# A hybrid encoder trunk on one core: weight-sum transfers issued behind bias rows, one convolution tile's taps behind the key selection, and the last scaling reordered

## The chip, the cores and the metric

The kernel runs on one core of a Trainium2 chip. The metric is the device time of one execution in microseconds, the median of several runs. The core has five engines that work side by side, each through its own queue in order: PE (TensorE, matrix products), DVE (VectorE, elementwise work), ACT (ScalarE, functions such as tanh and exp), POOL (GpSimd, here mostly the issuer of transfers) and SP (SyncE, also an issuer of transfers). SBUF is the on-chip memory, PSUM holds the results of matrix products, DRAM is the memory off the core. 16 DMA engines carry all transfers.

## The reference

The input is 512 positions of width 2048, with 16 meta tokens in front, so 528 columns. Two residual layers follow, each behind an RMS norm, and a final RMS norm whose gain is one number per channel.

```python
# even layer: one projection, two groups of heads
u = glu_v * sigmoid(glu_g)                       # 1024 channels
u = causal_depthwise_conv(u, width 31) + conv_b  # 31 taps per channel
a_out = silu(layer_norm(u)) * silu(gate_a)
score = sum_h wi * relu(qi_h . ki)               # 16 indexer heads
keys  = top 128 admissible keys per query        # chunk-causal
p     = softmax(q_lat . c + relative bias, over the selected keys)   # 8 heads
b_out = (p c w_uv) * silu(gate_b)
h = h + concat(a_out, b_out) @ w_out
# odd layer: gated linear recurrence, 16 heads, then h = h + (...) @ w_out
out = rms_norm(h, final_norm_gain)[16:]
```

## The kernel before

Activations lie in SBUF with channels on the 128 partitions and positions along the free dimension, so a width of 2048 is 16 tiles. A product is done three times to keep precision (high part with high part, high with low, low with high: L177, L178, L179). Weights come as blocks of 512 KB, loaded by SP (L144), and are split into a high part on ACT (L148) and a low part on DVE (L149). A projection of 128 output channels is a "stripe"; its result stands in PSUM (three buffers named mps) and is moved out by DVE with the norm's factor (`evac`, L185).

The order of each engine's queue is fixed when the program is built. A planner simulates the program and issues what is ready by priority bands: weight preparation, then evictions, then side work (scores, selection, attention), then the convolution, then all else in the order of the text. `issue_after(x)` adds a tie: what the block issues on x's own engine is queued behind x.

**Even layer.** The list `EVEN` (L46) gives the order of the text. `g` is a convolution tile: two stripes, the gated input u (L550, two buffers), then 31 taps on DVE (L554 and 30 times L556), each over 528 columns. `s` is one tile of two indexer heads: a stripe, two transfers of query halves by POOL (L506), small products, and DVE adds the weighted scores to four masks (L520). `k` is the selection for one block of 128 queries, on DVE: 16 times a maximum of eight and a replacement (L528, L529), then the mask is written (L530, L531). `h` is one attention head: two stripes, then `attend`. `n` is the layer norm over the eight convolution tiles.

**Attention.** For each of four query blocks `softmax` takes a tile L (three buffers). POOL loads the bias rows into it (L578), and adds the mask by an accumulating transfer (L580), which waits until the rows have landed and the mask is there. PE makes the logits (L587), DVE adds L and finds the extreme (L589), ACT takes the exponential and the scaling (L593, L596), PE transposes (L605, L609), ACT copies (L606, L610), and PE multiplies by the values (L612). A fifth, small block of 16 meta positions has bias rows of 1 KB and no mask.

**Weight sums.** The output projections use a seven-product form that needs sums of weight blocks. These are made by transfers in DRAM: `copy` steps and accumulating `add` steps of 512 KB each. For the even layer 16 copies (`plain_steps`) go out on SP during `g` and `s`; 48 further steps (`steps`: 16 first adds, then copies and adds, L247 and L249) go out on POOL during the heads.

**End.** The odd layer's output projection runs in 56 turns of 24 products. `add` puts results onto the residual h2; `finish` squares a finished half tile on ACT (L1114) and adds the square into a running sum (L1117). When all 16 tiles of the first half of the positions are complete, `final(0)` makes the norm's factor rsp in PSUM and scales tile by tile on DVE (L1151: h2 times the channel's gain times rsp), in four groups of four tiles. The groups stand between later turns by an order written out by hand (`tail`): two groups at once, one after the third last turn, one after the second last. `final(1)` follows after the last turn with all 16 tiles of the second half, through products, logarithm and exponential (L1131, L1132, L1134, L1136), and SP stores the output (L1153).

Of the kernel before, what the change touches and what calls it, by code (L numbers as in the profile page):

```python
# [14 lines left out]
AF = mybir.ActivationFunctionType  # L15
# [27 lines left out]
         "wiT": "ei", "ki": "ei", "rt": "ei", "m8": "ei",  # L43
         "mask0": "ei", "mask1": "ei", "mask2": "ei", "mask3": "ei"}

EVEN = "g0 s0 g1 s1 g2 s2 g3 s3 s4 s5 s6 s7 k0 k1 k2 k3 h0 h1 h2 g4 g5 h3 g6 h4 h5 g7 n0 h6 h7".split()  # L46

STAGE = [("gt", 3)] * 3 + [("gb", 2)] * 2 + [("qh", 2), ("mb", 2), ("mb", 2)]

# [23 lines left out]
def trunk_kernel(ctx: ExitStack, tc: tile.TileContext, x: bass.AP, w: bass.AP, wukv: bass.AP,  # L73
# [192 lines left out]
    def some_steps(todo, n, behind):  # L266
        with tc.issue_after(behind.ins):
            for _ in range(min(n, len(todo))):
                sum_step(*todo.pop(0))
# [224 lines left out]
    def scores(j):  # L494
        ps = stripe(S_QI + j, X0, wide=False)
        some_steps(plain_steps, 1, loaded[0])

        qab = E.tile([128, 2 * SEQ], F32R, name=("uh", "ul")[j % 2], bufs=1)
        qa, qb = qab[:, :SEQ], qab[:, SEQ:]
        ql = epools["ei"].tile([128, SEQ], F32R, name="ql", bufs=1)  # L500
        lo, up = slice(0, 64), slice(64, 128)
        with band(EVAC):
            for q, hi, lw, hf, other in ((qa, qa, ql, lo, up), (qb, ql, qb, up, lo)):
                S.activation(hi[hf], ps[0][0][hf], AF.Copy)
                V.tensor_tensor(lw[hf], ps[0][0][hf], hi[hf].bitcast(F32), op=OP.subtract)
                G.dma_start(q[other], ql[hf])  # L506
        with band(SIDE):
            for t in range(NB):
                for hh in range(2):
                    h, W = 2 * j + hh, wk(t)  # L510
                    q = (qa, qb)[hh]
                    qs = slice(128 * t, 128 * (t + 1))
                    for s0, s1 in (((0, W),) if W <= 512 else ((0, HT), (HT, W))):
                        p = ps1()
                        se = max(s1, s0 + 256)
                        P.matmul(p[:, :se - s0], q[:, qs], kih[:, s0:se], start=True, stop=False)  # L516
                        P.matmul(p[:, :se - s0], q[:, qs], kil[:, s0:se], start=False, stop=True)
                        r = et([128, T], F32, "sq", 3)
                        S.activation(r[:, :s1 - s0], p[:, :s1 - s0], AF.Relu)
                        V.scalar_tensor_tensor(M[t][:, s0:s1], r[:, :s1 - s0], wiT[:, t, h:h + 1],  # L520
                                               M[t][:, s0:s1], op0=OP.mult, op1=OP.add)

    def select(t):

        with band(SIDE):
            for _ in range(TOPK // 8):
                m8 = et([128, 8], F32, "m8", 2)
                V.max(m8, M[t])  # L528
                V.match_replace(M[t], m8, M[t], TAKEN)  # L529
            V.tensor_scalar(M[t], M[t], -2e38, NEG, op0=OP.is_gt, op1=OP.mult)  # L530
            V.memset(M[t][:64, wk(t) - 64:], NEG)  # L531


    Z = []
# [1 line left out]
    def glu(i):  # L536
        ps = stripe(S_GLU + 2 * i, X0)
        some_steps(plain_steps, 1, loaded[0])
        g = et([128, T], F32, "gt", 3)
        with band(EVAC):  # L540
            evac(g, ps, rstd0)
            S.activation(g, g, AF.Tanh, scale=0.5)
        ps = stripe(S_GLU + 2 * i + 1, X0)
        some_steps(plain_steps, 1, loaded[0])
        v = et([128, T], F32, "gt", 3)
        u = et([128, CW - 1 + T], F32, "u", 2)
        with band(EVAC):
            evac(v, ps, rstd0)
            V.memset(u[:, :CW - 1], 0.0)
            V.scalar_tensor_tensor(u[:, CW - 1:], g, 1.0, v, op0=OP.add, op1=OP.mult)  # L550
        z = et([128, T], F32, "z", 8)
        eng = V
        with band(CONV):
            eng.tensor_scalar(z, u[:, :T], col(V_CW + i * CW), col(V_CB + i), op0=OP.mult, op1=OP.add)  # L554
            for j in range(1, CW):
                eng.scalar_tensor_tensor(z, u[:, j:j + T], col(V_CW + i * CW + j), z,  # L556
                                         op0=OP.mult, op1=OP.add)
        Z.append(z)

    def gate(s, dst, X, rstd, wide=True):  # L560
# [12 lines left out]
    def attend(h, qh, gb, Kh, Vt):  # L573
        o = pso()

        def softmax(t, nq, q0, W):
            e = et([128, T], F32, "L", 3)
            G.dma_start(e[:nq, :W], bias_rows(h, q0, nq, 0, W))  # L578
            if t is not None:
                masked = G.dma_start(e[:, :W], M[t], accum_op=OP.add)  # L580
                some_steps(steps, 1 + t % 2, masked)
            L = e
            st = et([128, 4], F32, "st", 3)
            parts = ((0, W),) if W <= 512 else ((0, HT), (HT, W))
            for i, (s0, s1) in enumerate(parts):
                p = ps1()
                P.matmul(p[:nq, :s1 - s0], qh[:, q0:q0 + nq], Kh[:, s0:s1], start=True, stop=True)  # L587

                V.tensor_tensor_reduce(L[:nq, s0:s1], p[:nq, :s1 - s0], e[:nq, s0:s1], -1.0,  # L589
                                       st[:nq, i - 1:i] if i else BIG, OP.add, OP.min,  # L590
                                       st[:nq, i:i + 1])
            i = len(parts) - 1
            S.activation(L[:nq, :W], L[:nq, :W], AF.Exp, bias=st[:nq, i:i + 1], scale=-1.0,  # L593
                         accum_out=st[:nq, 2:3])
            V.reciprocal(st[:nq, 3:4], st[:nq, 2:3])
            S.activation(L[:nq, :W], L[:nq, :W], AF.Identity, scale=st[:nq, 3:4])  # L596
            return L

        for t in range(NB):
            q0, W = NM + 128 * t, wk(t)  # L600
            L = softmax(t, 128, q0, W)
            pt = et([128, 5, 128], F32, "pt", 2)
            p = ps1()
            for j in range(t + 1):
                P.transpose(p[:, j * 128:(j + 1) * 128], L[:, NM + 128 * j:NM + 128 * (j + 1)], ident)  # L605
            S.activation(pt[:, 1:t + 2, :], p[:, :128 * (t + 1)], AF.Copy)  # L606

            p = ps1()
            P.transpose(p[:, :128], L[:, :128], ident)  # L609
            S.activation(pt[:, 0, :], p[:, :128], AF.Copy)  # L610
            for j in range(t + 2):
                P.matmul(o[:, 128 * t:128 * (t + 1)], Vt[:, j, :], pt[:, j, :],  # L612
                         start=j == 0, stop=j == t + 1)
        mb = et([128, T], F32, "mb", 2)
        V.tensor_tensor(mb[:, NM:], o, gb[:, NM:], op=OP.mult)
        L = softmax(None, NM, 0, NM)
        p = ps1()
        P.transpose(p[:NM, :NM], L[:NM, :NM], ident[:NM, :NM])
        pt = et([128, 5, 128], F32, "pt", 2)
        V.tensor_copy(pt[:NM, 0, :NM], p[:NM, :NM])  # L620
        p = ps1()
        P.matmul(p[:, :NM], Vt[:NM, 0, :], pt[:NM, 0, :NM], start=True, stop=True)
        V.tensor_tensor(mb[:, :NM], p[:, :NM], gb[:, :NM], op=OP.mult)
        Q.dma_start(mbd[h], mb)
# [37 lines left out]

    for step in EVEN:
        what, i = step[0], int(step[1:])
        if what == "n":
            rz = layer_norm()
        else:
            {"g": glu, "s": scores, "k": select, "h": head}[what](i)


    MA = []
# [419 lines left out]
    acc2 = keep.tile([128, T], F32, name="rstd1", bufs=1)[:, :SEQ]  # L1091
    done = [0, 0]


    tail = []

# [7 lines left out]
    def finish(n, c):  # L1104

        cs = slice(c * HS, (c + 1) * HS)
        h2, a2 = H2[n][:, cs], acc2[:, cs]
        done[c] += 1
        sq = last = None
        if done[c] == 1:  # L1110
            S.activation(a2, h2, AF.Square)
        else:
            sq = tmp()
            last = S.activation(sq, h2, AF.Square)  # L1114
            if done[c] < KT:
                with tc.issue_after(tail[-1].ins) if tail else ExitStack():
                    ins = V.tensor_tensor(a2, a2, sq, op=OP.add)  # L1117
                if tail:
                    tail.append(ins)
        if done[c] == KT:  # L1120
            pending.append((sq, last))

    def final(c, behind=None):
# [14 lines left out]
        for g, size in enumerate((1, 1, 2, 2, 2, 2, 2, 2, 2) if c else (2,) * 8):  # L1138
# [9 lines left out]
            o = o[:, :size * HS].rearrange("p (n t) -> p n t", n=size)  # L1148
            with tc.issue_after(tail[-1].ins) if c == 0 and g else ExitStack():
                for i in range(size):  # L1150
                    tail.append(V.scalar_tensor_tensor(o[:, i, :], H2[at + i][:, tk], col(V_GF + at + i), rsp,  # L1151
                                                       op0=OP.mult, op1=OP.mult))
            Q.dma_start(out[at:at + size, :, tk].rearrange("n p t -> p n t"), o)  # L1153
            at += size
            if c == 0 and g % 2:
# [8 lines left out]
    for at, (pr, m) in enumerate(turns):  # L1164
# [7 lines left out]
        with band(EVAC):  # L1172
# [28 lines left out]
            else:  # L1201
                add(n1, 0, o, OP.subtract)
                finish(n1, 0)
            if at in (len(turns) - 3, len(turns) - 2):
                next(scaled)
    with band(EVAC):
        list(final(1))
# [90 lines left out]
```

## Time and profile before

| what | value |
|---|---|
| median of 3 runs | 1917.92 us (1917.48 to 1917.95) |
| the profiled execution | 1922.07 us |
| its span, first to last instruction | 1920.3 us |
| PE busy | 1897.4 us (99%) |
| DVE busy | 1424.0 us (74%) |
| ACT busy | 868.8 us (45%) |
| POOL busy | 181.9 us (9%) |
| mean granted PE clock | 0.997 |

The profile shows one execution. Its time is longer than the median, so differences are read within it. Busy time of PE is modelled at the ends of instructions, since products are pipelined. Issuing a transfer is not counted as busy time of SP; the rows of POOL show its issuing of transfers. A wait that the profile puts down to an engine is the one that came last by its records.

### The profile page before, as it was taken

The numbers are of one execution on the slowest core, as the hardware profiler recorded it, in microseconds if no ns is written. First come the engines' busy times: TensorE is split into PE (matmuls) and PEld (weight loads), VectorE is DVE, ScalarE is ACT, GpSimd is POOL, SyncE is SP. The second block draws the span as 40 slices with busy tenths as digits, with TensorE's granted clock in tenths as the row PEclk, the third lists the DMA queues.
The fourth block names the chain that finished last, engine by engine and source line by source line (L and its number), as shares of the span: only waits on it lengthen the run. The fifth ranks groups of instructions, "written<-read, shape, count | busy, mean of one in ns | idle before, by whom it ended". The sixth has DMA issues, their size and how long they took to land.

```text
span 1920.3 us, 36442 instructions
## 1 busy us (share of the span) xinstructions
PE 1897.4 (99%) x14806; PEld 1790.5 (93%) x14806; DVE 1424.0 (74%) x2724; ACT 868.8 (45%) x1515; POOL 181.9 (9%) x298
## 2 busy tenths in 40 slices
PE   9999999999999999999999999999999999999997
PEld 8999899899989999999999999999999988889996
DVE  6699989997548459687777777777777765558767
ACT  6332442234433555456455554545555443225443
POOL 1000000122222121002001000000100000000000
PEclk9999999999999999999999999999999999999999
DMA  6444334576777567566544444444444423334665
GB/s 233 137 136 137 127 94 138 137 183 181 185 192 187 156 183 245 194 225 220 145 130 128 131 129 122 121 121 132 132 131 125 121 78 99 99 109 158 210 223 169
DMA packets 84504, 292.89 MB, mean 153 GB/s; under 512 B 11312, under 2 KB 19032, under 8 KB 83312
## 3 DMA queue, kind: packets, MB, share of 16 engines
q1 hardware_dynamic: 60896, 204.37, 31.8%
q0 software_dynamic: 23152, 86.01, 19.3%
q8 instruction: 116, 1.90, 0.4%
q14 instruction: 52, 0.43, 0.1%
q10 hardware_dynamic: 288, 0.19, 0.0%
HBM read 271.42 MB, written 78.33 MB: 182 GB/s over the span
## 4 chain that ended last, share of the span: by engine, by line
PE 91%; issue 5%; DVE 2%; DMA 1%; POOL 1%; ACT 1%; SPq 0%; DVEq 0%; POOLq 0%; ACTq 0%
PE mps L179 23%; PE mps L177 23%; PE mps L178 23%; PE s L177 3%; PE s L178 3%; PE s L179 3%; PE po L612 1%; PE s L850 1%; PE s L849 1%; PE s L587 1%; PE s L851 1%; PE po L972 1%; PE po L971 1%; PE s L516 1%; PE s L968 1%
## 5 line engine op out<-in xcount | busy, mean ns | idle before, releaser
L177 PE MATMUL mps<-xh,wh 128*128 128x264 f32 (+2 forms) x3088 | 957.4, 310 | 3.1 <-DVE gt L185 2.7
L179 PE MATMUL mps<-xh,wl 128*128 128x264 f32 (+2 forms) x3088 | 956.7, 310 | 0.0
L178 PE MATMUL mps<-xl,wh 128*128 128x264 f32 (+2 forms) x3088 | 954.0, 309 | 0.0
L177 PEld LDWEIGHTS mps<-xh,wh 128*128 128x128 f32 x3088 | 582.6, 189 | 32.2 <-DVE gt L185 2.8
L178 PEld LDWEIGHTS mps<-xl,wh 128*128 128x128 f32 x3088 | 581.9, 188 | 29.4 <-issue 0.6
L179 PEld LDWEIGHTS mps<-xh,wl 128*128 128x128 f32 x3088 | 581.6, 188 | 27.2
L148 ACT ACTIVATE wh<-w 128x1024 fp32r<-128x1024 f32 x337 | 357.1, 1060 | 537.3 <-PE mps L178 407.5
L149 DVE TENSOR_TENSOR wl<-w,wh 128x1024 fp32r<-128x1024 f32 x337 | 412.4, 1224 | 150.4 <-ACT wh L148 143.7
L556 DVE SCALAR_TENSOR_TENSOR z<-u,vec,z 128x528 f32<-128x528 f32 x240 | 180.7, 763 | 2.6
L177 PE MATMUL s<-xh,wh 128*128 128x256 f32 (+1 forms) x400 | 113.1, 283 | 0.0
L178 PE MATMUL s<-xl,wh 128*128 128x256 f32 (+1 forms) x400 | 113.0, 283 | 0.0
L179 PE MATMUL s<-xh,wl 128*128 128x256 f32 (+1 forms) x400 | 112.9, 282 | 0.0
L185 DVE TENSOR_TENSOR gt<-mps,rstd 128x264 f32<-128x264 f32 (+1 forms) x80 | 38.4, 482 | 66.9 <-PE mps L179 66.2
L845 ACT ACTIVATE qhm<-q 128x256 f16<-128x256 f32 x128 | 52.0, 418 | 56.4 <-DVE q L947 44.2
L178 PEld LDWEIGHTS s<-xl,wh 128*128 128x128 f32 x400 | 75.4, 189 | 0.6 <-issue 0.6
L177 PEld LDWEIGHTS s<-xh,wh 128*128 128x128 f32 x400 | 75.6, 189 | 0.0
L179 PEld LDWEIGHTS s<-xh,wl 128*128 128x128 f32 x400 | 75.5, 189 | 0.0
L249 POOL DMA_DIRECT2D ws<-in_w_dram x64 | 61.8, 1045 | 109.8 <-DMA ws<-ws 67.4
L932 DVE COPY_PREDICATED A<-msk,s 128x256 f32<-128x256 uint8 x96 | 46.9, 488 | 27.5 <-PE s L851 27.0
L846 DVE SCALAR_TENSOR_TENSOR qlm<-q,qhm 128x256 f16<-128x256 f32 x128 | 53.1, 425 | 15.9 <-ACT qhm L845 15.7
L580 POOL DMA_DIRECT2D L<-mask x32 | 28.6, 895 | 234.0 <-DMA L<-bdram 145.3
L589 DVE CUSTOM_DVE_ANT_0 L<-s,L 128x144 f32<-128x144 f32 (+4 forms) x40 | 15.2, 381 | 44.9 <-PE s L587 23.6
(448 smaller groups left out, 2894.9 us busy)
## 6 DMA issues: line engine op xcount, KB each, us to landing
w<-in_w_dram SPq DMA_DIRECT2D x275, 512.0 KB, 3.6
ws<-in_w_dram POOLq DMA_DIRECT2D x80, 512.0 KB, 6.5
w<-ws SPq DMA_DIRECT2D x64, 512.0 KB, 3.6
ws<-ws POOLq DMA_DIRECT2D x32, 512.0 KB, 5.4
ws<-in_w_dram SPq DMA_DIRECT2D x16, 512.0 KB, 5.1
sq<-mbd POOLq DMA_DIRECT2D x16, 264.0 KB, 3.8
on<-h1d SPq DMA_DIRECT2D x14, 256.0 KB, 5.0
z<-in_x_dram SPq DMA_DIRECT2D x8, 264.0 KB, 4.8
```

The lines of the kernel that those rows point to most:

```text
L148: S.activation(uh, used, AF.Copy)
L149: V.tensor_tensor(ul, used, uh.bitcast(F32), op=OP.subtract)
L177: P.matmul(o, hi[:, ws], xh, start=start and k == 0, stop=False)
L178: P.matmul(o, hi[:, ws], xl, start=False, stop=False)
L179: issued.append(P.matmul(o, lo[:, ws], xh, start=False, stop=stop and k == len(X) - 1))
L185: V.tensor_tensor(dst[:, sl.start - o:sl.stop - o], p[:dst.shape[0]], rstd[:dst.shape[0], sl], op=OP.mult)
L249: return G.dma_start(wsum[pair, m], src, accum_op=OP.add, max_dma_last_dim=4096)
L556: eng.scalar_tensor_tensor(z, u[:, j:j + T], col(V_CW + i * CW + j), z, op0=OP.mult, op1=OP.add)
L580: masked = G.dma_start(e[:, :W], M[t], accum_op=OP.add)
L845: S.activation(hi, src, AF.Copy, scale=scale)
L846: V.scalar_tensor_tensor(lo, src, scale, hi, op0=OP.mult, op1=OP.subtract)
L932: V.copy_predicated(A.rearrange("p b (n a m) -> p b n a m", a=2, m=mm)[:, :, :, 1, :], msk[:, li - 1 + i:li + i, :].rearrange("p b (n m) - ...
```

## The change

Three edits. First, the selection of weight-sum steps moves: `softmax` issues them behind the bias rows of its block and ahead of the mask's transfer, two in the third block and one in each other (five per head instead of six), and the last four score tiles issue two each. Second, the fourth convolution tile (`LATER = 3`) writes its u as before, but its taps become a step of their own, `c3`, behind the selection, tied to the last mask's last instruction. Third, the final gain is multiplied into h2 on ACT when a half tile is finished, except in the last two tiles of each half; the final scaling of the others is then a plain product with rsp, and the fourth group of the first half moves from behind the second last turn to behind the last.

```diff
-EVEN = "g0 s0 g1 s1 g2 s2 g3 s3 s4 s5 s6 s7 k0 k1 k2 k3 h0 h1 h2 g4 g5 h3 g6 h4 h5 g7 n0 h6 h7".split()
+EVEN = "g0 s0 g1 s1 g2 s2 g3 s3 s4 s5 s6 s7 k0 k1 k2 k3 c3 h0 h1 h2 g4 g5 h3 g6 h4 h5 g7 n0 h6 h7".split()
...
     def scores(j):
         ps = stripe(S_QI + j, X0, wide=False)
         some_steps(plain_steps, 1, loaded[0])
+        if j >= 4:
+            some_steps(steps, 2, loaded[0])
...
-            V.memset(M[t][:64, wk(t) - 64:], NEG)
+            chosen.append(V.memset(M[t][:64, wk(t) - 64:], NEG))
...
+        U0[i] = u
+        if i != LATER:
+            convolve(i)
+    def convolve(i):
+        u = U0[i]
         z = et([128, T], F32, "z", 8)
-        with band(CONV):
+        with band(CONV), tc.issue_after(chosen[-1].ins) if i == LATER else ExitStack():
...
-            G.dma_start(e[:nq, :W], bias_rows(h, q0, nq, 0, W))
+            rows = G.dma_start(e[:nq, :W], bias_rows(h, q0, nq, 0, W))
             if t is not None:
-                masked = G.dma_start(e[:, :W], M[t], accum_op=OP.add)
-                some_steps(steps, 1 + t % 2, masked)
+                some_steps(steps, 2 if t == 2 else 1, rows)
+                G.dma_start(e[:, :W], M[t], accum_op=OP.add)
...
+        if done[c] < KT - 1:
+            S.activation(h2, h2, AF.Identity, scale=col(V_GF + n))
+        else:
+            ungained[c].append(n)
         if done[c] == KT:
             pending.append((sq, last))
...
-                    tail.append(V.scalar_tensor_tensor(o[:, i, :], H2[at + i][:, tk], col(V_GF + at + i), rsp,
-                                                       op0=OP.mult, op1=OP.mult))
+                    if at + i in ungained[c]:
+                        tail.append(V.scalar_tensor_tensor(o[:, i, :], H2[at + i][:, tk], col(V_GF + at + i), rsp,
+                                                           op0=OP.mult, op1=OP.mult))
+                    else:
+                        tail.append(V.tensor_tensor(o[:, i, :], H2[at + i][:, tk], rsp, op=OP.mult))
...
-            if at in (len(turns) - 3, len(turns) - 2):
+            if at in (len(turns) - 3, len(turns) - 1):
                 next(scaled)
```

## Rows read from the trace of the kernel before

**Rows 1.** The page, first part: busy us, share, instructions.

```profile
PE 1897.4 (99%) x14806; PEld 1790.5 (93%) x14806; DVE 1424.0 (74%) x2724; ACT 868.8 (45%) x1515; POOL 181.9 (9%) x298
```

**Rows 2.** PE's waits in the whole span: us in total, times, longest.

```profile
PE s L605 <- ACT L L596: 3.7, 2, 2.8
PE mps L177 <- DVE gt L185: 2.7, 5, 0.6
```

**Rows 3.** Busy time by engine, 336 to 384 us; then clock, DMA share, GB/s.

```profile
336.00:384.00 48.00, 44.40 (x354) 42.96 (x352) 44.78 (x90) 12.76 (x22) 7.96 (x11) 1.00 0.57 137
```

**Rows 4.** PE's timeline at 573 us (start, us, idle before), and a stretch's clock.

```profile
573.87 0.47 PE L605 MATMUL s<-ident,L 128*128 128x128 f32 x1 [2.80 <-ACT L L596]
...
574.00:577.00 3.00, 3.00 (x12) 2.59 (x13) 2.96 (x5) 1.96 (x4) 2.77 (x5) 0.57 0.53 91
```

**Rows 5.** POOL's timeline, 480 to 570 us: a mask, two sums, rows.

```profile
482.29 0.89 POOL L580 DMA_DIRECT2D L<-mask  x1 [5.25 <-DMA L<-bdram]
...
516.08 2.04 POOL L249 DMA_DIRECT2D ws<-in_w_dram  x2
517.15 1.54 POOL L578 DMA_DIRECT2D L<-bdram  x1
```

**Rows 6.** Transfers: median us to landing, 40 to 260, then 480 to 610 us.

```profile
L<-bdram POOLq DMA_DIRECT2D x1, 72.0 KB, 2.4
...
L<-bdram POOLq DMA_DIRECT2D x3, 72.0 KB, 9.5
```

**Rows 7.** The chain that ended last: start, us, what.

```profile
558.85 7.87 DMA L<-bdram
...
567.01 4.34 DMA L<-mask
```

**Rows 8.** Timelines of PE and DVE at the end.

```profile
1905.24 0.28 PE L179 MATMUL s<-xh,wl 128*128 128x256 f32 x1
...
1902.20 0.75 DVE L1100 TENSOR_TENSOR on<-on,s 128x256 f32<-128x256 f32 x2
...
1907.42 0.87 DVE L1151 SCALAR_TENSOR_TENSOR xl<-on,vec,s 128x256 f32<-128x256 f32 x2
1908.20 0.41 DVE L1100 TENSOR_TENSOR on<-on,s 128x256 f32<-128x256 f32 x1
1910.78 0.87 DVE L1151 SCALAR_TENSOR_TENSOR gt<-h,vec,s 128x256 f32<-128x256 f32 x2 [2.17 <-ACT s L1136]
```

**Rows 9.** Groups by line, 1895 to 1921 us: busy, mean ns.

```profile
L1151 DVE SCALAR_TENSOR_TENSOR xh<-on,vec,s 128x256 f32<-128x256 f32 x6 | 2.6, 476 | 0.0
...
L1100 DVE TENSOR_TENSOR on<-on,s 128x256 f32<-128x256 f32 x6 | 2.3, 416 | 1.0 <-PE s L179 1.0
```

**Rows 10.** Stretches of the output, columns as in rows 3.

```profile
1912.00:1914.00 2.00, 0.00 (x0) 0.00 (x0) 2.00 (x7) 0.00 (x0) 0.00 (x0) 0.50 0.71 236
1914.00:1918.00 4.00, 0.00 (x0) 0.00 (x0) 3.13 (x9) 0.00 (x0) 0.00 (x0) 0.50 1.01 332
```

**Rows 11.** ACT's groups by line, 1776 to 1890 us: busy, mean ns, idle before.

```profile
L148 ACT ACTIVATE wh<-w 128x1024 fp32r<-128x1024 f32 x40 | 42.4, 1061 | 60.7 <-PE s L178 29.1 <-issue 17.4 <-PE mps L178 14.2
L1114 ACT ACTIVATE t<-on 128x256 f32<-128x256 f32 x21 | 8.5, 405 | 0.9 <-DVE on L1195 0.9
```

**Rows 12.** Taps (L556) in two stretches; DVE's timeline around the selection.

```profile
250.00:365.00 115.00, 0.00 (x0) 1.00 0.42 112
365.00:400.00 35.00, 19.61 (x27) 1.00 0.77 203
...
261.21 0.90 DVE L520 SCALAR_TENSOR_TENSOR mask<-sq,wiT,mask 128x144 f32<-128x144 f32 x2
...
367.82 0.11 DVE L531 MEMSET mask<- 64x64 f32 x1
...
393.91 0.70 DVE L550 SCALAR_TENSOR_TENSOR u<-gt 128x528 f32<-128x528 f32 x1
```

**Rows 13.** DVE's waits in the whole span for a mask's transfer.

```profile
DVE L L589 <- DMA L<-mask: 13.8, 6, 5.0
```

More of the change, by code (lines that the diff above doesn't have):

```diff
@@ L530, in select @@
             V.tensor_scalar(M[t], M[t], -2e38, NEG, op0=OP.is_gt, op1=OP.mult)
-            V.memset(M[t][:64, wk(t) - 64:], NEG)
+            chosen.append(V.memset(M[t][:64, wk(t) - 64:], NEG))
+    chosen = []
     Z = []
@@ L550, in glu @@
             V.scalar_tensor_tensor(u[:, CW - 1:], g, 1.0, v, op0=OP.add, op1=OP.mult)
+        U0[i] = u
+        if i != LATER:
+            convolve(i)
+    U0 = {}
+    LATER = 3
+    def convolve(i):
+        u = U0[i]
         z = et([128, T], F32, "z", 8)
-        eng = V
-        with band(CONV):
-            eng.tensor_scalar(z, u[:, :T], col(V_CW + i * CW), col(V_CB + i), op0=OP.mult, op1=OP.add)
+        with band(CONV), tc.issue_after(chosen[-1].ins) if i == LATER else ExitStack():
+            V.tensor_scalar(z, u[:, :T], col(V_CW + i * CW), col(V_CB + i), op0=OP.mult, op1=OP.add)
             for j in range(1, CW):
-                eng.scalar_tensor_tensor(z, u[:, j:j + T], col(V_CW + i * CW + j), z,
-                                         op0=OP.mult, op1=OP.add)
+                V.scalar_tensor_tensor(z, u[:, j:j + T], col(V_CW + i * CW + j), z,
+                                       op0=OP.mult, op1=OP.add)
         Z.append(z)
@@ L667, in trunk_kernel @@
         else:
-            {"g": glu, "s": scores, "k": select, "h": head}[what](i)
+            {"g": glu, "s": scores, "k": select, "h": head, "c": convolve}[what](i)
     MA = []
@@ L1092, in trunk_kernel @@
     done = [0, 0]
+    ungained = [[], []]
     tail = []
```

## The prediction

> **What bounds the kernel now.** The page's first part comes first: PE is busy for 1897.4 of 1920.3 us [rows 1]. No part of the change adds or removes a matrix product, so what it can move is the 22.9 us in which PE is idle, and PE time at a low clock. The list of PE's waits says where to look in the middle: PE waits for a softmax tile (L605) twice, 3.7 us, and for an eviction (L185) five times, 2.7 us [rows 2]. The table by stretches shows that 336 to 384 us holds 3.60 us of idle PE (48.00 less 44.40) [rows 3]. That is stall 1, the time in which the selection of keys ends. Stall 2 is one gap of 2.80 us at 573.87 us [rows 4]. After it the granted clock averages 0.57 over 3 us, where 0.5 is the lower level, 1.2 GHz, and 1.0 the upper, 2.4 GHz [rows 4]; before, PE had been idle for those 2.80 us. The 3 us did 0.57 x 3 = 1.7 us of work, so 1.3 us went with the clock: stall 2 costs 2.80 + 1.3 = 4.1 us. The remainder lies at the start, which the change does not touch, and at the end: PE's last product issues at 1905.24 us, yet the last addition on DVE starts at 1908.20, the final scaling at 1910.78, and the span ends at 1920.3 [rows 8].
>
> The profiled execution took 1922.07 us, of which 1.77 lie outside its span; the median without a profile is 1917.92, 4.15 us less. I take the differences below from the profiled span and subtract them from the median. The 4.15 us are about the size of stall 2, so the stall may be smaller in plain executions; that is rival B.
>
> **The end.** DVE works without a gap worth naming from the first group of scaled tiles to the last addition, in an order written out by hand; two short waits for ScalarE's squares move with it. A scaling step of today (L1151) takes 476 ns, a tensor_tensor with one PSUM operand (L1100) 416 ns [rows 9]. Two in a row take 0.87 and 0.75 us [rows 8], so the repeat costs 0.87 - 0.476 = 0.39 and 0.75 - 0.416 = 0.33 us, 0.06 less each. (1) Ahead of the last addition stand twelve scaled tiles of the first half that become plain products: 12 x 0.06 = 0.7 us. (2) The fourth group, four tiles, moves behind the last addition: 4 x 0.39 = 1.6 us leave the path. The last addition starts 2.3 us earlier, at 1905.9. PE's last product issues at 1905.24 and lasts 0.28 [rows 8], so 1905.5 is the floor and PE is not late. What follows is a chain through ScalarE and PE of 1910.78 - 1908.20 = 2.58 us, in which DVE today sits idle for 2.17 [rows 8]; the moved group, two products and two old steps, 1.4 us, fits in it. Its two output transfers go to SP's queue ahead of those of the second half. (3) In the second half 14 of 16 steps become 0.06 us cheaper, 0.8 us on DVE, but the DMA engines are at a share of 1.01 and 332 GB/s from 1914 to 1918 [rows 10]. The second half's output is 16 x 128 x 256 x 4 bytes = 2.1 MB, 6.3 us at that rate; between 1912 and 1914 the share was 0.71 [rows 10], so at most 0.29 x 2 = 0.6 us of room is there to fill. I take 0.5, bounds 0 and 0.6. (4) The gains move to ScalarE: 28 activations like the square on the same 128x256 half, 0.41 us each, 11 us over 1760 to 1905. Cover: between 1776 and 1890 ScalarE waits 60.7 us ahead of its weight conversions alone [rows 11]. If the cover were gone, 0.41 us would show where the weights are late; I take 0. Sum of the end: 2.3 + 0.5 = 2.8 us, bounds 1.6 (the moved group alone) and 3.2.
>
> **The weight sums.** Today POOL issues, for each softmax block: bias rows, a wait until they have landed, the mask added to them, then one or two sum transfers of 512 KB, then the next block's rows. At 516.08 two sums, at 517.15 the next rows right behind [rows 5]. A load of 72 KB of bias rows lands in 2.4 us before the sums begin and in 9.5 us while they run [rows 6]: rows queue behind sums. From the mask issue at 482.29 to that at 567.01, 84.7 us, POOL issues masks for eight blocks and 12 sums and does little else than wait for rows [rows 5, 7], and the last of them is what stall 2 hangs on: rows issued at 558.85 take 7.87 us, the mask 4.34, and then DVE, ScalarE and PE go on at once [rows 7].
>
> After the change the sums go out behind a block's own rows, so POOL's wait covers rows that stand in front of these sums, and the sums run during that wait, the mask's issue and its start. 8 of the 48 sums leave the heads for the last four score tiles, so a head issues 5 instead of 6. The queue holds the same bytes, less a sixth of the sums. Per block POOL now takes 84.7 / 8 = 10.6 us, and 9.5 of that is a wait for rows. One sum fewer per head is worth about (9.5 - 2.4) / 2 = 3.5 us (an estimate: half of what one or two sums add to a landing), 7 us over the two heads before stall 2, more than its 2.80. So I let stall 2 go whole: 4.1 us, bounds 0 and 4.1. What is late next is the mask, which now stands behind the sums: rival D.
>
> The eight moved sums are issued by POOL, while the tie in the code is to a load that SP issues; it ties only instructions of the same engine, so they go where the planner finds POOL free once their copies exist. They share POOL's queue with the 128 KB query halves of the scores; at worst one half lands 7.1 us later (9.5 - 2.4 [rows 6]). PE has no gap there. I take 0.
>
> **The fourth tile's taps.** Today the four early convolutions' taps are done by 250 us: none runs from 250 to 365 [rows 12]. The selection begins when the last scores have been added to the first mask at 261.21 and ends at 367.82 [rows 12]. With no taps beside it, moving taps away does not shorten it, and it cannot start before the scores. So I give this part no gain at stall 1 (bounds 0 and 3.6). It puts 31 taps, 31 x 0.73 = 23 us of DVE (19.61 / 27 each [rows 12]), behind 367.9, where DVE is dense already. Two prices are possible. An eviction is late once more, as the L185 gaps: 2.7 / 5 = 0.5 us [rows 2]; I take one. And the sixth tile's input u, written at 393.91 [rows 12], needs the buffer of the fourth, free when its taps are done: at 27 taps in 35 us that is 31 x 35 / 27 = 40 us after 367.9, at 408, up to 14 us later. A next projection has the third of three gt buffers meanwhile, so I take 0, with 14 as a far end that the range does not hold.
>
> **The sum.** 2.8 + 4.1 - 0.5 = 6.4 us. 1917.92 - 6.4 = 1911.5; a profiled span would be 1913.9.
>
> **Rivals.**
> B, stall 2 is only in the profiled execution, or it moves to another block: the end's 2.8 us remain, 1915.1. For it: the 4.15 us between profile and median. Against it: 84.7 us of POOL waiting are not made by one late transfer.
> C, stall 1 goes as well, because fewer DVE operations early let scores and the first masks come sooner: 6.4 + 0.5 + 3.6 = 10.5 us, 1907.4. For it: DVE is 44.78 of 48 us busy there [rows 3]. Against it: the taps lay elsewhere. That is also the case in which the taps' move does what its name says; in A it does nothing.
> D, the other side: the mask behind the sums. The place is POOL's queue in the heads, where a mask lands behind one or two sums, 3.5 to 7.1 us later. DVE today waits for a mask in only 6 of 32 blocks, 13.8 us [rows 13]. If just these 6 grow by 3.5 to 7.1 us, DVE waits 21 to 43 us more, and PE sees 3.7 / 13.8 = 27% as today, 5.7 to 11.5 us. Against the end's 2.8 that gives 1920.8 to 1926.6, 1923 in the middle. It decides once the masks' slack, three L tiles deep, is below one sum. Against it: where POOL paced the heads, rows and mask together wait for the same bytes as before.
> On D's side stands a rule of the Trainium skill, page "DMA: Bandwidth & Descriptors", section "Two DMAs through the same engine are not ordered": descriptors of one queue on one DMA engine start in order. By that rule alone a mask would start behind every sum issued before it, in all 32 blocks, which is D; the trace agrees for bias rows (2.4 against 9.5 us [rows 6]), and no row of it shows a mask behind a sum.
>
> **How the numbers follow.** Chances: A 0.45 (own range 1909.5 to 1913.8), B 0.27 (1914.1 to 1916.5), C 0.12, D 0.13, anything else 0.03. The time is A's, 1911.5. The range 1906.8 to 1918.5 holds A, B and C and leaves D out. 0.2% is 3.8 us, about what a measurement of this kernel can tell from no change: faster means below 1914.1, which is A and C, 0.57; within is B and the mild part of D, 0.34; slower 0.09.
>
> **What would show it.** Right: no gap above 1 us at L605 on PE near 500 to 600 us, and the granted clock there at 1.00; bias rows landing below 6 us; masks landing in more than their 4.34 us; the last addition's start within 0.6 us of PE's last product, and 2.3 us less from that product to the final scaling; second-half steps of 416 ns, with DMA at a share of 1.0 through the output. Wrong: PE waits for L605 of more than 3.7 us in sum, or a POOL chain of rows and masks that again ends in one (D); PE waits at L185 between 390 and 470 us (the taps); a selection that ends well before 367.8 (C).

## The result, and the profile after

The changed kernel takes 1938.32 us (median of 4 runs, 1930.40 to 1939.16) against 1917.93 for the kernel before on the same chip (4 runs, 1917.48 to 1918.50): a ratio of 1.0097, 95% interval 1.0070 to 1.0123. It is 20.4 us slower where 6.4 us less were forecast. Its profiled execution took 1939.16 us with a span of 1937.4, which is 17.1 more than the span before (1920.3). In one run below (all sums tied) two of eleven executions, of 3102 and 4797 us, were in a slow state, and its median is that of the other nine.

Three stretches, of the kernel before and then after: length, busy time of PE, PEld, DVE, ACT and POOL, then granted clock, DMA share and GB/s.

```profile
48.00:192.00 144.00, 144.00 (x1010) 135.00 (x1009) 120.09 (x180) 47.04 (x77) 5.89 (x11) 1.00 0.41 137
384.00:480.00 96.00, 96.00 (x768) 93.48 (x767) 78.87 (x147) 36.51 (x81) 23.34 (x37) 1.00 0.70 182
528.00:624.00 96.00, 93.09 (x726) 90.05 (x726) 62.00 (x110) 36.33 (x68) 23.91 (x35) 0.98 0.76 190
```

```profile
48.00:192.00 144.00, 133.99 (x887) 124.42 (x886) 104.85 (x159) 43.20 (x71) 15.17 (x24) 0.94 0.58 163
384.00:480.00 96.00, 91.04 (x719) 88.59 (x718) 85.86 (x158) 32.51 (x71) 17.51 (x26) 0.98 0.59 154
528.00:624.00 96.00, 96.00 (x771) 93.45 (x771) 55.79 (x112) 38.82 (x88) 24.83 (x36) 1.00 0.71 172
```

The first row holds the loss. Between 48 and 192 us, long before the heads, PE was never idle and now stands for 10.0 us, at a mean clock of 0.94 (1.00 before). In the same stretch POOL's busy time rises from 5.89 to 15.17 us and the DMA share from 0.41 to 0.58: transfers are there that were not there before. PE loses 5.0 us more from 384 to 480. From 528 to 624, where stall 2 was, it is busy throughout at a clock of 1.00. The sum: 10.0 idle and 0.06 x 134 = 8.0 for the clock in the first stretch, 5.0 and 1.8 in the second, less 4.1 for stall 2 and 2.7 at the end (below), is 18.0, against 17.1 by the spans.

PE's waits after, in the whole span (total, times, longest), which stand against [rows 2]:

```profile
PE s L439 <- DMA z<-in_onehot_dram: 4.0, 1, 4.0
PE s L518 <- DMA uh<-ql: 3.2, 1, 3.2
PE s L618 <- ACT L L609: 3.2, 2, 1.8
PE s L518 <- DMA ul<-ql: 2.8, 1, 2.8
PE s L479 <- ACT Kh L468: 2.7, 1, 2.7
```

Three waits are new and end with a small transfer that POOL issues: the one-hot rows from which the bias rows are made (L439), and the query halves of two score tiles (L518). They make up the 10.0 us. L479 is a wait for an eviction of the keys. The 3.2 us at L618 lie at stall 1, between 336 and 384 us. POOL's timeline shows what stands in front of the three transfers:

```profile
50.72 0.88 POOL L249 DMA_DIRECT2D ws<-in_w_dram  x1 [1.16 <-DMA ws<-in_w_dram]
51.28 0.84 POOL L436 DMA_DIRECT2D z<-in_onehot_dram  x1
...
96.39 0.81 POOL L249 DMA_DIRECT2D ws<-in_w_dram  x1 [4.77 <-DMA ws<-in_w_dram]
97.33 1.15 POOL L508 DMA_DIRECT2D uh<-ql  x2
...
139.63 0.83 POOL L249 DMA_DIRECT2D ws<-in_w_dram  x1 [10.86 <-DMA ws<-in_w_dram]
140.46 1.16 POOL L508 DMA_DIRECT2D ul<-ql  x2
```

Each of the three goes out 0.6 to 0.9 us behind a weight sum of 512 KB. The one-hot rows come in three parts; PE waits for the last, and the part before it, issued 2.5 us behind the sum of 38.18 us, lands late too. Between 38 and 149 us POOL issues twelve sums (8 adds at L249, 4 copies at L247): the eight that moved to the scores, and four of the first head, which were tied to that head's bias rows, and the rows of its first three blocks go out at 61 to 62 us. How transfers land from 40 to 200 us, median in the last column, before and then after:

```profile
uh<-ql POOLq DMA_DIRECT2D x4, 128.0 KB, 2.6
ul<-ql POOLq DMA_DIRECT2D x2, 128.0 KB, 2.6
z<-in_onehot_dram POOLq DMA_DIRECT2D x2, 44.0 KB, 3.9
```

```profile
ws<-in_w_dram POOLq DMA_DIRECT2D x7, 512.0 KB, 8.6
uh<-ql POOLq DMA_DIRECT2D x4, 128.0 KB, 5.4
ul<-ql POOLq DMA_DIRECT2D x2, 128.0 KB, 8.4
z<-in_onehot_dram POOLq DMA_DIRECT2D x2, 44.0 KB, 8.2
```

Behind a sum the rows take 8.2 us instead of 3.9, and the halves of the second pair (`ul`) 8.4 instead of 2.6. The four named `uh` belong to two score tiles: the pair issued at 97.33 us lands in 8.3 us, the later pair in 2.6 as before, so their median is 5.4. In this profile each wait costs more than its idle time: the next rows show the clock after the three (third column from the end):

```profile
63.00:66.00 3.00, 3.00 (x9) 2.38 (x8) 0.00 (x0) 1.09 (x3) 1.55 (x3) 0.50 0.94 235
105.00:108.00 3.00, 2.10 (x9) 2.13 (x10) 0.90 (x2) 0.49 (x2) 0.00 (x0) 0.50 0.43 163
...
150.00:153.00 3.00, 3.00 (x17) 3.00 (x17) 2.49 (x6) 1.38 (x4) 0.00 (x0) 0.60 0.51 175
```

In the first and the last PE is busy throughout, but at 0.50 and 0.60, so at the lower level of 1.2 GHz for all or most of the time; in the middle one, 105.90 is the end of the wait, and the clock is 0.50. Such a fall does not follow every wait, as the run with only the eight early sums shows below.

The end, PE's and DVE's timelines, against [rows 8]:

```profile
1925.04 0.28 PE L179 MATMUL s<-xh,wl 128*128 128x256 f32 x1
```

```profile
1925.60 0.41 DVE L1115 TENSOR_TENSOR on<-on,s 128x256 f32<-128x256 f32 x1
1925.93 0.41 DVE L1174 TENSOR_TENSOR xh<-on,s 128x256 f32<-128x256 f32 x1
...
1926.98 0.47 DVE L1171 SCALAR_TENSOR_TENSOR xl<-on,vec,s 128x256 f32<-128x256 f32 x1
1928.18 0.75 DVE L1174 TENSOR_TENSOR gt<-h,s 128x256 f32<-128x256 f32 x2 [0.72 <-ACT s L1155]
```

The last addition now starts 0.56 us behind the last product's start (2.96 before), the fourth group lies in the wait that follows it, and from the last product to the final scaling it is 3.14 us instead of 5.54. To the end of the span it is 12.36 (1937.4 - 1925.04) instead of 15.06.

### The profile page after: what moved, and what is told of

Read it like the earlier page. It is cut to its first block, busy times and chain, and to the rows that moved or that the text cites. A ratio compares the mean times of both kernels' runs of the same rounds, so it can differ in the third digit from the quotient of the medians.

```text
span 1937.4 us, 36468 instructions
## 1 busy us (share of the span) xinstructions
PE 1904.0 (98%) x14806; PEld 1796.0 (93%) x14806; DVE 1420.6 (73%) x2724; ACT 883.2 (46%) x1543; POOL 182.1 (9%) x298
## 4 chain that ended last, share of the span: by engine, by line
PE 78%; DVE 2%; DMA 1%; ACT 0%; issue 0%; DVEq 0%
PE mps L179 20%; PE mps L177 20%; PE mps L178 20%; PE s L177 3%; PE s L178 3%; PE s L179 3%; PE po L625 1%; PE s L600 1%; PE s L863 1%; PE s L862 1%; PE s L864 1%; PE po L985 1%; PE po L984 1%; PE s L981 1%; DMA w<-in_w_dram 1%; PE s L479 0%
## 5 line engine op out<-in xcount | busy, mean ns | idle before, releaser
L148 ACT ACTIVATE wh<-w 128x1024 fp32r<-128x1024 f32 x337 | 357.2, 1060 | 517.7 <-PE mps L178 401.7
L185 DVE TENSOR_TENSOR gt<-mps,rstd 128x264 f32<-128x264 f32 (+1 forms) x80 | 38.3, 480 | 62.3 <-PE mps L179 61.6
L249 POOL DMA_DIRECT2D ws<-in_w_dram x64 | 54.1, 866 | 186.5 <-DMA ws<-in_w_dram 115.6
L522 DVE SCALAR_TENSOR_TENSOR mask<-sq,wiT,mask 128x264 f32<-128x264 f32 (+3 forms) x80 | 37.3, 494 | 22.8 <-ACT sq L521 22.4
L521 ACT ACTIVATE sq<-s 128x264 f32<-128x264 f32 (+3 forms) x80 | 29.1, 393 | 51.0 <-PE s L519 46.2
```

The lines of the kernel that those rows point to most:

```text
L148: S.activation(uh, used, AF.Copy)
L185: V.tensor_tensor(dst[:, sl.start - o:sl.stop - o], p[:dst.shape[0]], rstd[:dst.shape[0], sl], op=OP.mult)
L249: return G.dma_start(wsum[pair, m], src, accum_op=OP.add, max_dma_last_dim=4096)
```

## The experiments

Each run was timed beside the kernel before on the same chip; times are medians, ratios are with their 95% interval. The first four take the change apart.

**The end alone.** The third edit on the kernel before, nothing else.

> The kernel before with the third edit alone (gains on ScalarE, plain products, fourth group behind the last turn). Theory 1 (POOL's early weight sums make the loss, the end gains what was forecast): 1917.9 - 2.8 = 1915.1 us, with 2.6 us less from PE's last product to the final scaling and nothing else moved. Rival (the gains on ScalarE delay weight conversions): 1917 to 1919, with PE waits for L148 above the 0.4 us of before.

1915.67 us; before 1919.05; 0.9983 (0.9974 to 0.9992). The end is worth 3.4 us, near the 2.8 forecast. In its profile stall 2 is smaller without having been touched (PE busy 94.86 of 96.00 from 528 to 624, clock 1.00).

**The taps alone.** The second edit only.

> The kernel before with the second edit alone (fourth convolution tile's taps behind the selection). Theory 1: within 1 us of 1917.9, the selection's end within 3 us of 367.8. Rival 2 (the taps behind the selection make the loss between 288 and 480 us, where the changed kernel's PE is idle for 9.2 us against 3.6): 1921 to 1924.

1920.52; before 1919.05; 1.0009 (1.0000 to 1.0017).

```profile
384.00:480.00 96.00, 93.67 (x739) 91.29 (x738) 85.86 (x154) 32.77 (x72) 19.07 (x30) 0.98 0.64 168
528.00:624.00 96.00, 96.00 (x770) 93.67 (x769) 61.67 (x118) 41.04 (x87) 24.55 (x36) 1.00 0.79 192
```

In the profiles the small loss of 1.5 us is a difference of two things: PE loses 2.33 us and some clock from 384 to 480, the new wait at L479, and stall 2 is gone in the second row, where before lost 2.91 us.

**The sums alone.** The first edit only.

> The kernel before with the first edit alone (sums behind bias rows, eight of them in the score tiles). Theory 1: 1936 to 1942 us, with PE idle for 8 to 11 us between 48 and 192 us behind query halves and one-hot rows on POOL's queue, and a low clock there. Rival 2: 1930 to 1935, the remainder being the taps. A second rival (the three edits hurt only together): below 1925.

1933.18 (four runs, 1925.40 to 1934.79); before 1919.05; 1.0066 (1.0048 to 1.0085). The sums alone lose 14.1 us; most of the loss is in the first edit. The four executions lie 9 us apart, and their mean clocks go with them, 0.997 in the fastest and 0.994 in the two longest. The profile caught the fastest: there PE waits for the one-hot rows (3.5 us) and the first pair of halves (1.5), and not for the second pair, which went out 1.57 us behind its sum.

**Sums behind the rows, none in the scores.** Only the order within the heads is changed, six sums a head.

```diff
-                masked = G.dma_start(e[:, :W], M[t], accum_op=OP.add)
-                some_steps(steps, 1 + t % 2, masked)
+                some_steps(steps, 1 + t % 2, rows)
+                G.dma_start(e[:, :W], M[t], accum_op=OP.add)
```

> The kernel before with the sums behind the bias rows in the heads, six per head as before, none in the score tiles. The first head's rows go out at 57 us, so four of its sums are free to go early. Theory 1: four early adds cost about a third of twelve early sums, 5 to 8 us, less stall 2: 1919 to 1924 us. If only the eight in the score tiles did the harm: 1913 to 1918, and no early stall.

1925.11; before 1919.05; 1.0038 (1.0025 to 1.0052). Even without the eight, 6.1 us are lost: the first head's four sums go out early by themselves, and one of them stands ahead of a pair of query halves, for which PE waits 3.5 us. Not all of the loss is at this place: from 288 to 384 us PE is busy for 90.44 us, 2.0 less than before.

```profile
89.34 0.84 POOL L249 DMA_DIRECT2D ws<-in_w_dram  x1 [25.48 <-DMA ws<-in_w_dram]
90.25 1.15 POOL L506 DMA_DIRECT2D uh<-ql  x2
```

**Another issuer for the small transfers.** The changed kernel, with the query halves, the keys' copies, the one-hot rows and the writes of the bias table made from them issued by ScalarE, so that they share no queue with the sums.

```diff
-                G.dma_start(q[other], ql[hf])
+                S.dma_start(q[other].bitcast(F32), ql[hf].bitcast(F32))
...
-            G.dma_start(oh[:32, :352], onehot[:, o:o + 352])
+            S.dma_start(oh[:32, :352], onehot[:, o:o + 352])
```

> The changed kernel with all three edits, in which ScalarE's queue instead of POOL's issues the transfers that stand between the early weight sums: the keys' copies, the one-hot rows, the bias table's writes and the query halves of the scores. The sums keep their places. Queue theory (small transfers stand behind 512 KB sums in POOL's queue): query halves land in 2.5 to 4 us instead of 8.3, PE's idle time between 48 and 192 us falls from 10.0 to below 1 us, the clock there is 1.00, and the time is 1917 to 1922 us. Contention theory (the same 16 DMA engines are loaded, whichever queue issues): halves land in 6 us or more, half or more of the idle time stays, 1926 us or more.

1930.09; before 1918.56; 1.0059 (1.0043 to 1.0075). How they land from 40 to 200 us:

```profile
uh<-ql ACTq DMA_DIRECT2D x4, 128.0 KB, 7.0
ul<-ql ACTq DMA_DIRECT2D x2, 128.0 KB, 5.9
z<-in_onehot_dram ACTq DMA_DIRECT2D x2, 44.0 KB, 4.9
```

From a queue of their own the pair of halves near 96 us still takes 7.5 us (the other two named `uh` 3.3) and the pair at 136 us 5.9, against 2.6 before; the one-hot rows take 4.9 against 3.9. PE's idle time from 48 to 192 falls only from 10.0 to 6.5 us. So for the halves the place in POOL's queue is the smaller part of the delay, and for the rows the larger. What remains without it points to the 16 DMA engines, which all queues share; no run shows that share by itself, since the profile lists ScalarE's queue as another kind than POOL's (`hardware_dynamic`, `software_dynamic`), and the run changes both. In time the run loses 11.5 us where the changed kernel loses 20.4.

**All sums tied.** The changed kernel, but the eight sums of the scores are tied to that tile's query halves and the first head's to its masks, all on POOL, so that none can go ahead.

```diff
-        if j >= 4:
-            some_steps(steps, 2, loaded[0])
...
-                G.dma_start(q[other], ql[hf])
+                moved = G.dma_start(q[other], ql[hf])
+        if j >= 4:
+            some_steps(steps, 2, moved)
```

> The changed kernel with all three edits, but the eight sums of the score tiles tied behind that tile's query halves on POOL (the tie names an instruction of POOL's own queue), and the first head's sums behind its masks, as before the change; the other heads' sums stay behind bias rows. Theory (the loss is the sums that went early, not sums behind rows): no idle PE between 48 and 192 us, and the time is the end's gain plus the taps' small loss, 1914 to 1918 us. If sums ahead of the masks in the heads are a loss of their own: above 1920.

1920.39 (1920.85 over all eleven executions); before 1918.56; 1.0007 (0.9998 to 1.0016). From 48 to 192 us PE is busy throughout at a clock of 1.00, and of the loss of 20.4 us 1.8 are left:

```profile
48.00:192.00 144.00, 144.00 (x1007) 134.91 (x1007) 120.31 (x180) 46.96 (x78) 5.91 (x11) 1.00 0.42 136
```

What early sums cost is shown by this: the same bytes by the same issuer, later. The time lies above 1920, where sums ahead of the masks were expected to be a loss of their own; the next run, which keeps these sums and is faster than before, shows that they are not.

**Tied sums and the end, taps where they were.**

> As the run with tied sums, without the second edit (the fourth tile's taps stay where they were). Theory: 1.5 us below that run, 1912 to 1916 us, no wait of PE for the value products (L479) between 384 and 480 us, and no gap above 1 us at the transposes between 500 and 624 us. If the taps' move helps once the sums are in place: above that run.

1914.71; before 1918.56; 0.9981 (0.9971 to 0.9991). Against the run above only the taps differ: 5.7 us, where 1.5 were expected. The profiled spans differ by 6.2 us (1919.3 and 1913.1): from 384 to 480 us the run above has 2.46 us of idle PE and a clock of 0.98 over 93.54, 4.3 together, where this one has neither, and from 192 to 288 us it has 1.8 us less of busy PE, with a wait of 1.5 us for ScalarE at the scores (L521).

**Sums behind the rows, the first head's behind its masks, none in the scores, and the end.**

> The kernel before with the third edit and the sums behind bias rows in heads 1 to 7 (the first head's behind its masks), six per head, none in the score tiles, no taps moved. Against the run without taps it differs only in the eight sums that go out during the scores. If the order within a block is what counts: within 1 us of that run, 1912 to 1916. If the eight sums fewer in the heads are what counts: 1915 to 1918, as the end alone.

1915.45; before 1918.56; 0.9979 (0.9970 to 0.9989). Its profile has no idle PE from 384 to 480 or from 528 to 624:

```profile
384.00:480.00 96.00, 96.00 (x769) 93.63 (x769) 78.86 (x146) 36.97 (x81) 23.59 (x37) 1.00 0.71 187
528.00:624.00 96.00, 96.00 (x767) 93.62 (x766) 65.04 (x115) 41.36 (x77) 21.51 (x31) 1.00 0.73 187
```

So sums behind rows do take stall 2 away, and yet the gain is 3.1 us, no more than the 3.4 of the end alone. Whether the eight sums fewer in the heads help stays open: 0.7 us between this run and the one above is within the spread of either.

**Sums and end, no taps' move.** The changed kernel without its second edit.

> The kernel after without the move of the taps: sums issued early, the end reordered. Theory 1 (the three edits add: sums +14, end -3.3 as each measured alone): 1929, some 9 us under the kernel after, with PE waiting for the one-hot rows and one query half between 48 and 192 us, and no wait at L479 near 440 to 470 us. Theory 2 (the moved taps and the early sums make each other worse, the taps' move costs far more when the sums are early than the 1.6 us that it costs alone): 1922 to 1927, more than 11 us under the kernel after. Theory 3 (the taps' move is nothing here, the early sums carry all of the loss): 1935 or more.

1928.48; before 1918.63; 1.0052 (1.0037 to 1.0067). The three edits do not add: -3.4 + 1.5 + 14.1 = 12.2, but 20.4 were measured. Sums and end together do (9.9 against 10.7), so it is the taps' move that costs some 10 us here (1938.32 - 1928.48) and 1.5 alone. Part of that can be seen in the profiles: alone it also took stall 2 away, which the sums have already taken here. Between 384 and 480 PE has 95.47 us in this kernel, at 1.00, and 91.04 at 0.98 in the changed one: 4.4 us idle and 0.02 x 91 = 1.8 of clock, 6.2 of the 8.9 us by which the spans differ (1937.4 - 1928.5). The remainder lies from 48 to 192 us, where the idle times are close (9.5 and 10.0 us) and the clock is 0.96 here and 0.94 there. As the next run shows, the clock differs that much after like waits, so this part need not be the taps'.

**Only the eight early sums.** The end, and eight free sums in the scores; the other forty behind the masks.

> The end reordered; the eight sums moved to the loads of the scores, free to go early; the other forty behind the masks of the heads, five per head. Theory 1 (each early sum costs alike; twelve of them cost 14, the first head's four cost 6): eight cost about 9, so 1924 to 1925. Theory 2 (what costs is only that the sums meet the one-hot rows and the first query half, which the first few sums suffice for): about 1921, one wait near 60 us or 106 us, none near 149 us. Theory 3 (the eight are not what costs, the first head's four are): 1916.

1928.85; before 1918.63; 1.0060 (1.0043 to 1.0076). None of the three theories gave this: eight sums lose as much as twelve. POOL's timeline says why:

```profile
50.23 0.89 POOL L249 DMA_DIRECT2D ws<-in_w_dram  x1 [0.98 <-DMA ws<-in_w_dram]
50.78 0.85 POOL L436 DMA_DIRECT2D z<-in_onehot_dram  x1
...
96.19 0.81 POOL L249 DMA_DIRECT2D ws<-in_w_dram  x1 [10.75 <-DMA ws<-in_w_dram]
97.35 1.16 POOL L508 DMA_DIRECT2D uh<-ql  x2 [0.35 <-DVE ql L507]
...
137.09 0.81 POOL L249 DMA_DIRECT2D ws<-in_w_dram  x1 [11.19 <-DMA ws<-in_w_dram]
138.07 1.15 POOL L508 DMA_DIRECT2D ul<-ql  x2 [0.18 <-issue]
```

Eight are enough to put one sum right ahead of each of the same three transfers. The loss goes with the number of waits that follow: one in the run with the first head's four sums (6.1 us); three here, 10.2 us lost although the end gains 3.4, so 13.6; and three in the run of sums and end, 13.2 in the same way.

The profile shows one thing more. The wait for the first pair ends at 105.97 us after 3.28 us, in the changed kernel at 105.90 after 3.24, yet here the clock stays at 1.00:

```profile
105.00:108.00 3.00, 2.03 (x16) 2.06 (x17) 1.13 (x3) 1.21 (x4) 0.00 (x0) 1.00 0.43 161
```

From 48 to 192 us PE is idle for 10.55 us at a mean clock of 0.98, in the changed kernel for 10.0 at 0.94. So waits that are alike in length can differ in what the clock adds to them.

**Taps written later.** All sums tied, `c3` behind the third head in the order of the text.

```diff
-EVEN = "... k2 k3 c3 h0 h1 h2 g4 ...".split()
+EVEN = "... k2 k3 h0 h1 h2 c3 g4 ...".split()
```

> The kernel after with the eight sums tied behind that tile's query halves and the first head's behind its masks (1920.9 before), and the fourth tile's taps written behind the third head instead of right behind the selection. Theory 1 (the taps cost because they stand in VectorE's queue ahead of the weight conversion that frees the buffer of the key and value load): the taps go later, the wait at L479 near 445 us goes, and the time comes to 1915 to 1917. Theory 2 (VectorE has no room for 21 us more anywhere behind the selection): the same 5 to 6 us are lost later, 1919 to 1922, with other waits between 480 and 620 us.

1919.82; before 1918.63; 1.0008 (0.9999 to 1.0017). It told nothing apart: from 420 to 440 us DVE does 15 taps as it did with all sums tied. The place in the text did not move them, and the wait at L479 stayed, 2.4 us.

**One sum instead of two at the wait.** With all sums tied, ACT's timeline ahead of the wait at L479 shows a weight conversion (L148) that waits for its load, and the fourth eviction of the keys (L468), which was ready, behind it:

```profile
441.79 0.40 ACT L468 ACTIVATE Kh<-s 128x264 f32<-128x264 f32 x1 [0.34 <-PE s L466]
447.22 1.06 ACT L148 ACTIVATE wh<-w 128x1024 fp32r<-128x1024 f32 x1 [5.04 <-DMA w<-in_w_dram]
448.18 0.37 ACT L468 ACTIVATE Kh<-s 128x264 f32<-128x264 f32 x1
```

The chain of waits goes on behind it: the load takes 9.49 us, beside two sums, and could go out only when DVE had freed its buffer, in a conversion queued behind a tap:

```profile
435.80 0.75 DVE z L569
436.54 1.15 DVE wl L149
437.71 9.49 DMA w<-in_w_dram
```

In this run the pair of sums goes out one block later, in the first head too.

```diff
-                    some_steps(steps, 2 if t == 2 else 1, rows)
+                    some_steps(steps, 2 if t == 3 else 1, rows)
```

> The kernel with all sums tied and the taps moved (1920.9), with the pair of sums that one tile of each head issues put one tile later: at 436 us one sum goes out instead of two. There the weight load that goes out at 437.7 lands 9.5 us later beside the two sums, ScalarE's conversion of it waits 5.0 us, and the fourth eviction of the keys stands behind it. Theory 1 (the load is late because of the two sums beside it): it lands in 4 to 6 us, the wait at L479 goes, 1915 to 1917. Theory 2 (the load is late because it goes out late, behind VectorE's tap and conversion, and one sum with the mask's and output's transfers fills the engines as well): it lands in 8 us or more, the wait stays, 1919 to 1921.

1917.76; before 1918.45; 0.9993 (0.9984 to 1.0002): 0.7 us below before where the run with all sums tied is 1.8 above, so 2.5 of the taps' 5.7 us. ACT's timeline:

```profile
444.76 1.06 ACT L148 ACTIVATE wh<-w 128x1024 fp32r<-128x1024 f32 x1 [3.35 <-DMA w<-in_w_dram]
445.72 0.37 ACT L468 ACTIVATE Kh<-s 128x264 f32<-128x264 f32 x1
```

The load goes out at 436.93 and lands by 444.76, so in 7.8 instead of 9.5 us; ACT waits 3.35 instead of 5.04, and PE at L479 0.8 instead of 2.5. Both theories hold a part: the second sum cost some 1.7 us of landing, and the rest is there with one sum too. Of the 4.0 us by which the spans differ (1919.3 and 1915.3), 1.35 lie from 192 to 288 us, where this profile lacks the wait of 1.5 us at L521; that part is not the load's.

## Why the prediction was wrong

**The step that failed** is the one on the eight moved sums: "they go where the planner finds POOL free once their copies exist ... at worst one half lands 7.1 us later ... PE has no gap there. I take 0." Its first half was right and should have led on. POOL is free from the first 40 us on, so the planner put the sums there, one ahead of each small transfer that PE needs next. Even the size was near (8.4 - 2.6 = 5.8 us for a half). What was wrong is the inference from no gap to no cost. That PE had no gap there says that the transfers were in time, not by how much; three delays became three stalls of 2.8 to 4.0 us, in the changed kernel's profile each with a stretch of low clock after it. The trace of before could have told the room:

```profile
90.06 1.15 POOL L506 DMA_DIRECT2D uh<-ql  x2 [31.04 <-DVE ql L505]
```

```profile
94.76 0.28 PE L516 MATMUL s<-kih,uh 128*128 128x256 f32 x1
```

The second of these halves goes out at 90.7 us and lands 2.6 later, at 93.3, and PE uses it at 94.76; the next pair lands at 130.5 and is used at 132.00. That is 1.5 us of room each, against landings that became 5.7 and 5.8 us longer. The last one-hot rows had 7.3 us (issued at 45.23, landed 3.9 later, used at 56.42), but they went out 6.0 us later and took 4.3 us longer.

**Overlooked** was the first head. Its sums were tied to masks, the first of which goes out at 284.23 us; tied to bias rows they depend on nothing later than some 60 us. The edit in the heads let the first four sums go 220 to 250 us earlier (57.72 to 119.64 in the run with this edit alone, 284.82 to 337.31 before), and this edit alone lost 6.1.

**Rival D** had the mechanism, a small transfer delayed by a sum, and not the place: it looked at masks in the heads, where each L tile has two others beside it, and the cost came where a query half has no spare. Its own sign did not come: after the change PE's waits at the transposes sum to 3.2 us (3.7 before) and lie at stall 1. Of the rule that stood with it, from the Trainium skill, page "DMA: Bandwidth & Descriptors", section "Two DMAs through the same engine are not ordered", the trace shows what fits: transfers issued right behind a sum on the same queue land in 8.2 to 8.4 us instead of 2.6 to 3.9. But in the run with another issuer the two pairs of halves still took 7.5 and 5.9 us, so order within one queue is not most of their delay. The same page, section "Issuing engines are not separate DMA queues", says that transfers of every issuer run on the same 16 engines and interleave there; that run agrees, as far as it goes.

**The taps** were mis-sized: 0.5 us was taken, for one late eviction, and with the sums tied they cost 5.7. The price was not at L185 there (in the changed kernel two such waits, 1.3 us, lie from 384 to 480 us). The wait for u was mis-sized too: the sixth tile's u is written at 432.46 us with all sums tied and at 394.47 without the taps' move, 38 us later where 14 was the far end, though no wait of PE ends on it. What PE waits for is another chain: DVE, denser by 23 us, frees a weight buffer later, its load goes out at 437.71 us instead of 433.01 and beside sums, and on ACT a conversion that waits for the load holds up an eviction that was ready.

**Stall 2** went, as forecast, in the profile: bias rows of 72 KB land in 2.2 us from 480 to 610 us instead of 9.5 [rows 6]. The working had read those 9.5 us of landing as POOL's wait in each of the 10.6 us per block; POOL's idle time ahead of these eight masks is 60.7 us in sum, 7.6 a block, and the term of 4.1 us did not rest on it. But 4.1 us were not to be had. The kernels in which it is gone and nothing else is lost, 1914.71 and 1915.45 us, gain 3.9 and 3.1 us on the kernel before, and the end alone gains 3.4. That is rival B for this term, as far as the times can tell. The profile of the end alone, which does not touch the stall, has 1.1 us of idle PE there instead of 2.9; how large it is in executions without a profile stays open.

**Stall 1** stayed (91.75 us of PE from 288 to 384, 92.40 before), as taken.

**The end** was right in its steps: last addition to 0.56 us of the last product's start, the moved group inside the wait for ScalarE, 2.40 us less to the final scaling (2.3 forecast) and 2.70 less to the end of the span (2.8; its upper bound of 3.2 is more than its parts give, 2.3 + 0.6). The second half's steps take 415 ns, and the output runs at a DMA share of 1.03 and 341 GB/s. Only ScalarE's new step is dearer than the square it was priced by, 0.51 against 0.41 us, and it hid all the same. Alone it makes the kernel faster by 0.17% (interval 0.08 to 0.26), and the versions that are faster than before all have it.

## What to carry to other kernels

Before background transfers are given freedom to go early, list the small transfers that will now go out beside them, and read from the trace how long each has lain landed before its user starts; an engine without a gap does not say that there is room (here it was 1.5 us). A tie says from when a transfer may go, so moving a tie from a late event to an early one moves work across the whole program, not only past its neighbour in the text. When parts of a change have been measured apart, allow for one stall being removed by two of them, whose gain is then counted twice.

## What the runs showed of the hardware

A 128 KB transfer that lands in 2.6 us with no sum beside it took 8.4 us behind one DRAM-to-DRAM sum of 512 KB, and 5.9 to 7.5 when another engine issued it. In the changed kernel waits of PE of 2.8 to 4.0 us were followed by rows of 3 us at a clock of 0.50 or 0.60; over 48 to 192 us the clock took 0.06 x 134 = 8.0 us, nearly as much as the 10.0 of the waits. But a wait of 3.28 us in the run with eight early sums was followed by a clock of 1.00, where one of 3.24 us, ending at the same point of the program, was followed by 0.50: with like waits the clock's cost from 48 to 192 us was 8.0 us in one profile and 0.02 x 133 = 2.7 in the other. On ScalarE a copy with a per-channel factor of 128x256 took 0.51 us, the square of the same shape 0.41 [rows 11].
